# Other numbers for the planner of the heads, four gate blocks early and four held back, and a bank of its own for the last product

## The chip, the cores and the metric

The kernel runs on one core of a Trainium2 chip. The metric is the device time of one execution in microseconds; smaller is better. Before the change the median of three runs is 1488.58 us (1488.05 to 1491.75). One further execution was profiled; every duration below comes from it.

The engines have short names: PE multiplies matrices (PEld is its loading of weights), DVE does vector work, ACT functions and copies, POOL general vector work, and SP issues the DMAs. Each engine takes its instructions in the order in which they were recorded and waits for semaphores in that order.

## The reference

One encoder block for 1024 tokens of width 1024, all in f32:

```
h = rmsnorm(x) * (1 + scale) + shift                # scale, shift, gate from c
bg, cg, ax, az, q, k, v, z, a_raw, b_raw, ga, gb = split(h @ w_in)
ya = (cg * dwconv3(bg * ax) * silu(az)) @ w_pa
q, k, v = silu(dwconv5([q, k, v])); q, k = l2norm(q), l2norm(k)
o = gated_delta(q, k, v, g, beta) forwards + the same backwards     # 8 heads of 128
yb = (rmsnorm(o) * gdn_norm_w * silu(z)) @ w_pb
merged = sigmoid(ga) * ya + sigmoid(gb) * yb
y = rmsnorm(x + gate * (merged @ w_o))
```

`gated_delta` is chunked, and in each chunk it needs the inverse of a unit lower triangular matrix, made from the products of the keys with each other.

## The kernel before

Each f32 product is made of three passes: the weights and the activations are split into a high part (`wh`, `hhi`) and a rest (`wl`, `hlo`), and PE adds hi·hi, lo·hi and hi·lo. A block of 128 columns of `w_in` is thus 48 matmuls of 512 columns, in two halves (`pp_q3_0`, `pp_q3_1` for q of head 3), 24 each. Its weights come by DMA (`wr`), ACT writes `wh`, and POOL subtracts to get `wl` (`load_weights`); an eviction by ACT takes the product from its bank of PSUM (`xpad`).

The program has three parts. First x is normalised and transposed, and the first products are made, to about 102 us of the profile. Then come the eight heads, to about 799 us. The rest is written out by hand: more gate blocks, four groups of Strassen-like pairs of blocks (each pair is seven products, S1 to S4, A11, A12 and A22) with one more pair for the columns of `gb` as the last, and the three products with `w_pa`, `w_pb` and `w_o`.

The heads are recorded by a planner (`Scheduler`). Each head has generators: `prep_k` makes the keys and the matrices N from `gram` (the products of the keys), and issues the inverse; `merge` doubles the inverse's blocks on PE (`psy`, `psu`, `pst`, `psz`, `psv`); `chain` runs the eight steps of the state in both directions (`cb`); `prep_q` and `head_out` do the rest. `chain` and `merge` have the first priority, `prep_k` the second. `fill` is a stream of projections (k, q, v and z of the heads) and eight gate blocks (`ga0` to `ga7`), whose matmuls stand wherever nothing of higher priority is due.

The inverse is the long stretch between gram and psy. DVE makes N and its transposes, DMAs take them through DRAM into a layout for POOL (`s1`, `E`), POOL does 60 small operations that each depend on the one before (`et` and `E`, thirty of each), DMAs bring the result back (`s2`, `N`, `Vb`), DVE and ACT transpose it (`N<-Vb`, `T`, `y`), and `psy` may start.

The planner keeps a time for each engine, estimates each operation's duration (`Engine.cost`), and adds a hop between an operation and one that depends on it: `HOPS['same']` if both are on one engine, other values otherwise. POOL's operations end 0.05 us later for those that depend on them than for the engine itself. It takes what can start first by these numbers; among what is waiting on one engine, priority decides. The numbers set only the order, since the hardware's semaphores hold the real dependences.

`fill` decides by `choose` when a gate block is due: `START` of the eight stand first, and the last blocks, at most `RESERVE`, are kept for places where no projection may go. With the numbers of before, six blocks stand early and two at the end.

In the last pair (`Pair`, `place = "last"`, order S2, S1, S3, A22, A11, A12, S4) each product accumulates in a bank given by its name, `BANK`; S1 and S4 share one of the pool `pc`, and A12 has a bank of `po`, a pool of two.

Of the kernel before, what the change touches and what calls it, by code (L numbers as in the profile page):

```python
# [8 lines left out]
F32 = mybir.dt.float32  # L9
F32R = mybir.dt.float32r  # L10
AF = mybir.ActivationFunctionType
ALU = mybir.AluOpType
# [9 lines left out]
NEG = -1.0e30  # L22

A_BG, A_CG, A_X, A_Z, Q0, K0, V0, Z0, G_A, G_B = (8 * i for i in range(10))
START = 6
RESERVE = 3
PLAIN = (0, 4)
LAST = 6
AHEAD = 5
HOPS = {'same': 0.15, 'other': 0.2, 'from pe': 0.4, 'to pe': 0.35}  # L30
ORDER = "x0 b x1 x2 x3 k0 a0 x4 x5 x6 x7 q0 a1 v0 a2 a3 a4 a5 a6 a7".split()
SPLIT = 2
XS = 'apvapvav'
# [1 line left out]
LW = "gg"  # L35
# [19 lines left out]
class Scheduler:  # L55
# [19 lines left out]
        self.prio = before  # L75

    def hop(self, a, b):
        return HOPS["same" if a == b else "from pe" if a == "pe" else "to pe" if b == "pe" else "other"]

    def after(self, engine, *ends):  # L80
        return max((t + self.hop(e, engine) for d in ends for e, t in d.items()), default=0.0)
# [178 lines left out]
class Engine:  # L260
# [5 lines left out]
    def cost(self, op, outs, ins, kw):  # L266

        n = outs[0].free_size() / 1000.0
        if self._name == "dma":
            size = min(outs[0].nbytes(), ins[0].nbytes())  # L270
            return max(0.4, size / 360e3), 2.4 + size / 500e3
        if self._name == "act":
            pointers = sum(isinstance(kw.get(k), bass.AP) for k in ("bias", "scale"))
            return 0.1 + 0.83 * n + 0.07 * pointers + 0.12 * (len(outs) > 1), 0.08
        if self._name == "pool":
            if ALU.pow in kw.values():
                return 1.7, 0.1
            return (0.31 + 1.95 * n if "tensor" in op else 0.06 + 0.7 * n), 0.05
        if op == "transpose":
            return 0.16 + 1.1 * n, 0.03  # L280
        both = sum(i.space != PSUM and i.free_size() == outs[0].free_size() for i in ins) > 1
        fast = op in ("tensor_copy", "tensor_scalar", "memset") and ins and ins[0].space != PSUM
        return 0.07 + 0.06 * (op == "scalar_tensor_tensor") + (0.66 if fast else 1.2 if both else 1.04) * n, 0.07

    def __getattr__(self, op):
        real = getattr(self._engine, op)
# [14 lines left out]
def block(ctx: ExitStack, tc: tile.TileContext, x, cT, wada, wadag, badaT, nwT, win, wab, cva, cvq,  # L301
# [3 lines left out]
    V, S, G, Q = (Engine(sched, n, e) for n, e in (("dve", nc.vector), ("act", nc.scalar), ("pool", nc.gpsimd),  # L305
                                                   ("dma", nc.sync)))

    def pool(name, bufs, **kw):
        return ctx.enter_context(tc.tile_pool(name=name, bufs=bufs, **kw))
# [5 lines left out]
    pc = pool("pc", 2, space=PSUM)  # L315
    po = pool("po", 2, space=PSUM)
# [24 lines left out]
    def ch(c, w=P):  # L341
        return slice(w * c, w * c + w)
# [13 lines left out]
    def tile_of(pl, shape, tag, name, bufs, dtype=F32):  # L356
        return "tile", pl, shape, tag, name, bufs, dtype

    def urgent():
        return sched.priority(0)  # L360
# [16 lines left out]
    def load_weights(pl, src, name, tag="w", spare=None):  # L377
        hi = yield tile_of(pl, [P, KT * P], f"{tag}hi", f"wh_{name}", 2, F32R)
        lo = yield tile_of(pl, [P, KT * P], f"{tag}lo", f"wl_{name}", 2, F32R)
        for q in range(2):  # L380
            if spare is None:
                raw = yield tile_of(wp, [P, 512], "wraw", f"wr_{name}_{q}", 2)
            else:
                if q == 0:
                    whole = yield staged(spare, f"wr_{name}")
                raw = whole[:, ch(q, 512)]
            with sched.priority(1):
                Q.dma_start(raw, src[:, ch(q, 512)])
                S.activation(hi[:, ch(q, 512)], raw, AF.Copy)
                (G if LW[q] == "g" else V).tensor_tensor(lo[:, ch(q, 512)], raw, hi[:, ch(q, 512)].bitcast(F32), ALU.subtract)  # L390
        weights[name] = hi, lo
        yield "mark", ("w", name)

    def loader(i=0, n=None):
        while n is None or i < n:
            yield "need", ("want", i)
            if wanted[i] is None:
                return
            yield from load_weights(wp, *wanted[i])
            i += 1  # L400
# [12 lines left out]
    def staged(tag, name, dtype=F32):  # L413
        return tile_of(hp, [P, T], tag, name, 1, dtype)
# [26 lines left out]
    with tc.tile_pool(name="st", bufs=1) as st:  # L441
# [172 lines left out]
        def first_weights():  # L614
            for n, name, spare in ((K0, "k0", "hlo5"), (Q0, "q0", "hhi4"), (V0, "v0", "hlo4")):
                yield "need", name
                yield from load_weights(wp if n == V0 else st, win[n], name, "w" if n == V0 else "f", spare)
            yield want(win[K0 + 1], "k1")
# [455 lines left out]
    def fill():  # L1074
# [14 lines left out]
        def choose():  # L1089
            share = (total - START - RESERVE) * (mains - len(jobs)) / mains + START  # L1090
            if gates and jobs and total - len(gates) < int(share):
                return gates.pop(0)
            if jobs and (len(gates) <= RESERVE or all(n in sched.done for n in jobs[0][3])):
                return jobs.pop(0)
            return gates.pop(0) if gates else None
# [18 lines left out]
    V, S, G, Q, PE = nc.vector, nc.scalar, nc.gpsimd, nc.sync, nc.tensor  # L1114

    def bank(pl, name):
        return pl.tile([P, 512], F32, tag="b", name=name)
# [11 lines left out]
    def product(w, mhi, mlo, half, name, order=tuple(range(KT))):  # L1129
        ps = bank((pp, pg)[half], f"pp_{name}_{half}")  # L1130
        for i, k in enumerate(order):
            wh, wl = (t[:, ch(i)] for t in w)
            sl = ch(half, 512)
            PE.matmul(ps, wh, mhi[k][:, sl], start=i == 0, stop=False)  # L1134
            PE.matmul(ps, wh, mlo[k][:, sl], start=False, stop=False)  # L1135
            PE.matmul(ps, wl, mhi[k][:, sl], start=False, stop=i == KT - 1)  # L1136
        return ps
# [31 lines left out]
    BANK = {"S2": pg, "A11": pp, "S1": pc, "S3": pg, "A12": pp, "A22": pg, "S4": pc}  # L1169
# [15 lines left out]
    class Pair:  # L1185
# [31 lines left out]
            self.ops[n] = hi, lo  # L1217

        def product(self, n):
            pl = po if (self.place, n) in (("first", "S4"), ("last", "A12")) else BANK[n]  # L1220
            first = pl not in self.banks
            if first:
                self.banks[pl] = bank(pl, f"ps_{self.name}_{n}")
            ps = self.banks[pl]
            hi, lo = self.ops.pop(n)
            for m in range(4):
                mh, ml = hop[RHS[n]][m]
                for i, (w, r) in enumerate(((hi, mh), (hi, ml), (lo, mh))):
                    PE.matmul(ps, w[:, ch(m)], r, start=first and m == i == 0, stop=m == 3 and i == 2,  # L1229
                              skip_group_check=True)  # L1230
            self.after(n, ps)
# [8 lines left out]
        def after(self, n, ps):  # L1240
            u = self.u
            if self.place == "last":
                if n in ("S2", "S3"):
                    self.temp({"S2": "u2", "S3": "u3"}[n], ps, None)
                elif n == "A11":
                    self.temp("e1", ps, None)
                    V.tensor_tensor(u["u3"], u["u3"], u["e1"], ALU.add)
                    self.consume(1, 1, self.banks[pc], u["u3"])
                    self.consume(1, 0, self.banks[pg], u["e1"])
                    V.tensor_tensor(u["u2"], u["u2"], u["e1"], ALU.add)  # L1250
                elif n == "A12":
                    self.consume(0, 0, ps, u["e1"])
                elif n == "S4":
                    self.consume(0, 1, ps, u["u2"])
                return
            first = self.place == "first"
            if n == "A11":
                self.temp("e1", ps, None)
            if n == ("S2" if first else "A11"):
                self.temp("u2", self.banks[pg], u["e1"])  # L1260
                if first:
                    V.tensor_tensor(u["u2"], self.banks[po], u["u2"], ALU.add)
            if n == "S3":
                self.temp("u3", ps, u["e1"])
                self.consume(1, 1, self.banks[pc], u["u3"])
            elif n == "A12":
                self.consume(0, 0, ps, None)
            elif n == "A22":
                self.consume(1, 0, ps, u["e1"])
            elif n == ("S1" if first else "S4"):  # L1270
                self.consume(0, 1, ps, u["u2"])
# [95 lines left out]
    for i, (p, n) in enumerate(steps):  # L1367
        if i + AHEAD < len(steps):
            q, k = steps[i + AHEAD]
# [139 lines left out]
    for n in range(2):  # L1509
        for t in range(8):  # L1510
            if n == 0:
                load_wo(1, t)
            pl = (pp, pg)[t % 2]
# [81 lines left out]
```

## Time and profile before

| | |
|---|---|
| median of three runs | 1488.58 us |
| profiled execution | 1486.97 us |
| its span on the core | 1485.2 us |
| mean granted clock of PE | 0.981 |
| first part ends, heads end | about 102 and 799 us |
| POOL, the 240 `E` and 240 `et` | 120.0 and 114.3 us |

The span is what the profile shows from the first instruction to the last. A row of a view names the line, the engine, the operation, and out<-in by the program's names without buffer numbers. An idle time is put down to the event that ended it. `engine, number` with an `x` behind it is busy time and the count of instructions; the granted clock is 1.00 at full speed.

### The profile page before, as it was taken

What the parts mean: (1) busy time and instruction counts of PE and PEld (TensorE: products, weight loads), DVE (VectorE), ACT (ScalarE), POOL (GpSimd) and SP (SyncE); (2) the same over time, 40 slices, a digit from 0 to 9 for tenths busy, and PEclk for the clock granted to TensorE, in tenths of its full rate; (3) what the DMA queues carried; (4) which work ended last, traced back from release to release, by engine and by line L of the source; (5) the groups of instructions that cost most, each with busy time, mean ns of one, the idle gap of its engine ahead of it and who ended that gap; (6) DMA issues with size and microseconds to landing.
All of it is one profiled execution on the core that took longest, in us unless ns stands there. A gap on an engine that the chain in (4) does not pass through costs nothing.

```text
span 1485.2 us, 22649 instructions
## 1 busy us (share of the span) xinstructions
PE 1402.8 (94%) x8526; PEld 1161.1 (78%) x8526; DVE 858.9 (58%) x1466; ACT 614.0 (41%) x1495; POOL 691.8 (47%) x864
## 2 busy tenths in 40 slices
PE   5799999899999999996899999999999899999998
PEld 4687878787878787875788877787878677788886
DVE  7959327467767657476525566565756446623335
ACT  5227728546565647464434323232222431222211
POOL 6103748462768473575404745454454312255301
PEclk9899999999999999997999999999999999999999
DMA  8204351312342412323112320303030557565502
GB/s 322 94 29 138 105 134 56 86 39 84 114 97 82 115 44 50 105 71 89 29 44 86 113 79 22 114 15 128 15 113 30 190 188 239 197 199 169 193 15 100
DMA packets 123582, 153.37 MB, mean 103 GB/s; under 512 B 74705, under 2 KB 75089, under 8 KB 123473
## 3 DMA queue, kind: packets, MB, share of 16 engines
q1 hardware_dynamic: 123184, 151.14, 32.0%
q8 instruction: 67, 1.10, 0.3%
q10 hardware_dynamic: 288, 0.79, 0.1%
q14 instruction: 43, 0.34, 0.1%
HBM read 122.40 MB, written 29.49 MB: 102 GB/s over the span
## 4 chain that ended last, share of the span: by engine, by line
PE 67%; DVE 12%; POOL 8%; ACT 5%; DMA 4%; issue 2%; SPq 1%; POOLq 0%; ACTq 0%; DVEq 0%
PE pp_ga L204 6%; PE cb L204 4%; PE pp_q L204 4%; PE pp_k L204 4%; PE ps_ax_S L1229 4%; PE ps_cg_S L1229 3%; POOL E L295 3%; POOL et L295 3%; PE o L204 3%; PE ps_bg_S L1229 3%; PE ps_az_S L1229 2%; PE pp_pb L1134 2%; PE pp_pb L1135 2%; PE pp_pb L1136 2%; PE fo L1501 2%
## 5 line engine op out<-in xcount | busy, mean ns | idle before, releaser
L295 POOL TENSOR_TENSOR E<-E,et 128x30 f32<-128x30 f32 (+7 forms) x240 | 120.0, 500 | 16.6
L295 POOL TENSOR_TENSOR et<-E 128x30 f32<-128x30 f32 (+7 forms) x240 | 114.3, 476 | 27.5 <-DMA E<-s 10.8
L295 ACT ACTIVATE vw<-cb,cols 128x128 f32<-128x128 f32 x112 | 34.9, 363 | 92.0 <-PE cb L204 91.8
L295 DVE SCALAR_TENSOR_TENSOR S<-S,exps,cb 128x128 f32<-128x128 f32 x96 | 29.2, 343 | 69.8 <-PE cb L204 69.5
L1126 POOL TENSOR_TENSOR wl_pa<-wr_pa,wh_pa 128x512 fp32r<-128x512 f32 x16 | 20.4, 1295 | 86.6 <-ACT wh_pa L1125 86.6
L295 ACT ACT_TABLE_LOAD x42 | 53.9, 1283 | 1.4 <-PEq L1590 0.8
L295 POOL TENSOR_TENSOR wl_ga<-wr_ga,wh_ga 128x512 fp32r<-128x512 f32 x16 | 23.2, 1455 | 65.9 <-ACT wh_ga L295 65.8
L204 PE MATMUL pp_z<-hlo,wh_z 128*128 128x512 f32 x128 | 53.1, 415 | 0.0
L204 PE MATMUL pp_z<-hhi,wh_z 128*128 128x512 f32 x128 | 52.9, 413 | 0.0
L204 PE MATMUL pp_z<-hhi,wl_z 128*128 128x512 f32 x128 | 52.6, 411 | 0.0
L204 PE MATMUL pp_ga<-hhi,wh_ga 128*128 128x512 f32 x128 | 51.2, 400 | 1.5 <-ACT xpad L295 1.5
L204 PE MATMUL pp_ga<-hhi,wl_ga 128*128 128x512 f32 x128 | 51.5, 402 | 0.0
L204 PE MATMUL pp_ga<-hlo,wh_ga 128*128 128x512 f32 x128 | 51.1, 399 | 0.0
L1134 PE MATMUL pp_pb<-bhi,wh_pb 128*128 128x512 f32 x128 | 50.6, 396 | 0.0
L1136 PE MATMUL pp_pb<-bhi,wl_pb 128*128 128x512 f32 x128 | 50.6, 395 | 0.0
L1135 PE MATMUL pp_pb<-blo,wh_pb 128*128 128x512 f32 x128 | 50.6, 395 | 0.0
L1134 PE MATMUL pp_pa<-yhi,wh_pa 128*128 128x512 f32 x128 | 50.5, 395 | 0.0
L1136 PE MATMUL pp_pa<-yhi,wl_pa 128*128 128x512 f32 x128 | 49.9, 390 | 0.0
L1135 PE MATMUL pp_pa<-ylo,wh_pa 128*128 128x512 f32 x128 | 49.9, 389 | 0.0
L204 PE MATMUL pp_q<-hhi,wl_q 128*128 128x512 f32 x112 | 46.7, 417 | 2.1 <-POOL wl_q L295 2.1
L295 DVE SCALAR_TENSOR_TENSOR r<-cb,negeg,vp 128x128 f32<-128x128 f32 x112 | 34.0, 344 | 23.7 <-PE cb L204 23.4
L295 DVE SCALAR_TENSOR_TENSOR qT<-xpad,cvq_t,qT 128x1024 f32<-128x1024 f32 x32 | 47.2, 1474 | 0.5
(806 smaller groups left out, 4660.7 us busy)
## 6 DMA issues: line engine op xcount, KB each, us to landing
wada<-in_wada SPq DMA_DIRECT2D x16, 512.0 KB, 7.1
D<-gr_d SPq DMA_DIRECT2D x16, 512.0 KB, 7.7
xt<-in_x SPq DMA_DIRECT2D x8, 512.0 KB, 7.6
wr_k<-in_win SPq DMA_DIRECT2D x16, 256.0 KB, 3.1
wr_q<-in_win SPq DMA_DIRECT2D x16, 256.0 KB, 3.8
wr_v<-in_win SPq DMA_DIRECT2D x16, 256.0 KB, 4.7
wr_ga<-in_win SPq DMA_DIRECT2D x16, 256.0 KB, 3.2
qg<-er_d SPq DMA_DIRECT2D x8, 512.0 KB, 5.3
```

The source lines that it names most:

```text
L204: getattr(self.pe, what)(out, *ins, **kw)
L295: self._sched.record(self._name, lambda: real(*args, **kw), outs, ins, cost, extra, table, op == "memset")
L1126: G.tensor_tensor(lo[:, ch(q, 512)], raw, hi[:, ch(q, 512)].bitcast(F32), ALU.subtract)
L1134: PE.matmul(ps, wh, mhi[k][:, sl], start=i == 0, stop=False)
L1135: PE.matmul(ps, wh, mlo[k][:, sl], start=False, stop=False)
L1136: PE.matmul(ps, wl, mhi[k][:, sl], start=False, stop=i == KT - 1)
L1229: PE.matmul(ps, w[:, ch(m)], r, start=first and m == i == 0, stop=m == 3 and i == 2, skip_group_check=True)
L1501: PE.matmul(ps, mhi[k][:, ch(t)], wl, start=False, stop=k == KT - 1)
```

## The change

The planner's numbers and two spots of code change; the arithmetic stays, apart from the order of one sum.

```
-START = 6
-RESERVE = 3
+START = 4
+RESERVE = 4
...
-HOPS = {'same': 0.15, 'other': 0.2, 'from pe': 0.4, 'to pe': 0.35}
+HOPS = {'same': -0.05, 'other': 0.2, 'from pe': 0.4, 'to pe': 0.35}
...
     def hop(self, a, b):
-        return HOPS["same" if a == b else "from pe" if a == "pe" else "to pe" if b == "pe" else "other"]
+        if a == b and a != "dma":
+            return HOPS["same"]
+        return HOPS["from pe" if a == "pe" else "to pe" if b == "pe" else "other"]
...
-        return 0.07 + 0.06 * (op == "scalar_tensor_tensor") + (0.66 if fast else 1.2 if both else 1.04) * n, 0.07
+        return 0.07 + 0.06 * (op == "scalar_tensor_tensor") + (0.66 if fast else 1.16 if both else 1.04) * n, 0.07
...
-                (G if LW[q] == "g" else V).tensor_tensor(lo[:, ch(q, 512)], raw, hi[:, ch(q, 512)].bitcast(F32), ALU.subtract)
+                with urgent():
+                    (G if LW[q] == "g" else V).tensor_tensor(lo[:, ch(q, 512)], raw, hi[:, ch(q, 512)].bitcast(F32), ALU.subtract)
...
-            pl = po if (self.place, n) in (("first", "S4"), ("last", "A12")) else BANK[n]
-            first = pl not in self.banks
+            own = (self.place, n) in (("first", "S4"), ("last", "A12"), ("last", "S4"))
+            pl = po if own else BANK[n]
+            first = own or pl not in self.banks
...
                     V.tensor_tensor(u["u2"], u["u2"], u["e1"], ALU.add)
+                    V.tensor_tensor(u["u2"], self.banks[pc], u["u2"], ALU.add)
```

Two dependent operations of one engine now have no gap in the plan (two DMAs count as different engines); a DVE operation on two SBUF tensors counts a little less; the `wl` subtraction has the first priority; and four gate blocks stand early, four are held back. In the last pair S4 no longer accumulates upon S1's bank but starts its own, and a DVE addition brings S1's sum into `u2`, which is later added to S4.

The planner moves much of the heads' order. Three places of it follow. The first is PE at the merge of head 7, where psy7 begins and psu7 follows it. Before, psy7 stood behind the last matmuls of z6, and up to psu7 there were only transposes of head 6's output (`otp6`):

```order
L204 MATMUL pp_z6_1_7412<-hhi7_621,wh_z6_6934 128x512
L204 MATMUL pp_z6_1_7412<-hlo7_622,wh_z6_6934 128x512
L204 MATMUL pp_z6_1_7412<-hhi7_621,wl_z6_6935 128x512
L204 MATMUL psy7_7550<-T64_7_7082,N0_7_6479 32x32
...
L204 MATMUL psy7_7550<-y64_7_7083,N1_7_6480 32x32
L204 MATMUL otp6_0_7589<-ident_72,vp6_6506 128x128 x4
L204 MATMUL otp6_1_7595<-ident_72,vp6_6506 128x128 x2
L204 MATMUL psu7_7599<-N0_7_6479,Vb7_7008 32x32 x2
```

Now the gate block `ga4` stands around it:

```order
L206 MATMUL pp_ga4_0_7498<-hlo1_106,wh_ga4_7396 128x512
L206 MATMUL pp_ga4_0_7498<-hhi1_102,wl_ga4_7397 128x512
L206 MATMUL pp_ga4_0_7498<-hhi2_103,wh_ga4_7396 128x512
L206 MATMUL psy7_7511<-T64_7_6877,N0_7_6367 32x32
...
L206 MATMUL psy7_7511<-y64_7_6878,N1_7_6368 32x32
L206 MATMUL pp_ga4_0_7498<-hlo2_107,wh_ga4_7396 128x512
L206 MATMUL pp_ga4_0_7498<-hhi2_103,wl_ga4_7397 128x512
L206 MATMUL pp_ga4_0_7498<-hhi3_104,wh_ga4_7396 128x512
L206 MATMUL pp_ga4_0_7498<-hlo3_108,wh_ga4_7396 128x512
L206 MATMUL pp_ga4_0_7498<-hhi3_104,wl_ga4_7397 128x512
L206 MATMUL pp_ga4_0_7498<-hhi4_509,wh_ga4_7396 128x512
L206 MATMUL psu7_7554<-N0_7_6367,Vb7_6876 32x32 x2
```

Six wide matmuls now stand between psy7 and psu7, and `ga4` to `ga7` go on beside the rest of merge 7 and chain 7.

The second place is ACT at the third and fourth gate block, early in the heads. `wh_ga3` is the high part of the weights of block 3, `xpad<-pp_ga2_1` the eviction of the second half of block 2, D the decay matrices of head 1. Before:

```order
L295 ACTIVATE xpad0_116<-pp_ga1_1_1228 128x512
L295 ACTIVATE sqj_884,kss1_902<-ktp1_0_1284 128x128 x4
L295 ACTIVATE wh_ga3_1294<-wr_ga3_0_1296 128x512
L295 ACTIVATE ktok1_901<-ktp1_1_1305 128x512
L295 ACTIVATE sqj_884,kss1_902<-ktp1_1_1305 128x128 x4
```

and now:

```order
L297 ACT_TABLE_LOAD
L297 ACTIVATE xpad1_117<-pp_ga2_1_1368 128x512
L297 ACT_TABLE_LOAD
L297 ACTIVATE D1_1_905<-D1_1_905,neggc_122 128x128
L297 ACTIVATE wh_ga3_1309<-wr_ga3_0_1311 128x512
L297 ACTIVATE wh_ga3_1309<-wr_ga3_1_1312 128x512
```

`wh_ga3` stood behind the eviction of block 1; it now stands behind that of block 2. On PE the matmuls of block 3 directly follow block 2's.

The third place is POOL in the inverse of head 3. Leaving out `E` and `et`, before there stood among its sixty operations:

```order
L295 MEMSET E3_3519 64x16
...
L295 TENSOR_TENSOR wl_v3_3645<-wr_v3_0_3646,wh_v3_3644 128x512
...
L295 TENSOR_TENSOR wl_z2_3902<-wr_z2_0_3903,wh_z2_3901 128x512
...
L295 TENSOR_TENSOR oss2_3922<-oss2_3922,pos_half_78 128x8
...
L295 TENSOR_TENSOR kss4_3906<-kss4_3906,pos_half_78 128x8
...
L295 TENSOR_TENSOR wl_q4_4026<-wr_q4_0_4027,wh_q4_4025 128x512
...
L295 MEMSET E3_3519 64x16 x2
```

and now:

```order
L297 MEMSET E3_3301 64x16
...
L297 TENSOR_TENSOR wl_v3_3555<-wr_v3_0_3556,wh_v3_3554 128x512
...
L297 MEMSET E3_3301 64x16 x2
L297 TENSOR_TENSOR wl_z2_3814<-wr_z2_0_3815,wh_z2_3813 128x512
L297 TENSOR_TENSOR wl_z2_3814<-wr_z2_1_3816,wh_z2_3813 128x512
L297 TENSOR_TENSOR oss2_3806<-oss2_3806,pos_half_78 128x8
L297 TENSOR_TENSOR kss4_3818<-kss4_3818,pos_half_78 128x8
L297 TENSOR_TENSOR wl_q4_3937<-wr_q4_0_3938,wh_q4_3936 128x512
```

Each `wl` comes in two halves, of which the second isn't shown where "..." stands. Before, six of these subtractions and two powers stood inside the inverse; now two subtractions do, and the others follow it. Between the last gram of head 3 and psy3 PE had 228 matmuls of 512 columns and 120 of 128; now it has 156 and 114. For heads 4 to 7 the new counts are 166 to 175 and 106, where they were 179, 197, 241 and 144 of the wide ones and 106 to 122 of the narrow.

## The prediction

> **What bounds the kernel now.** I read the page's first two parts, then the waits of PE, then windows cut where those waits lie, then the timeline at one wait and the chain of one head.
>
> ```profile
> span 1485.2 us, 22649 instructions
> PE 1402.8 (94%) x8526; PEld 1161.1 (78%) x8526; DVE 858.9 (58%) x1466; ACT 614.0 (41%) x1495; POOL 691.8 (47%) x864
> PEclk9899999999999999997999999999999999999999
> ```
>
> PE is busy for 1402.8 of 1485.2 us, no other engine for more than 58%. So time can only be won or lost in PE's idle 82.4 us and where its clock is down, above all near the 19th digit of the clock. The waits of PE say what it stood for:
>
> ```profile
> PE psz L204 <- ACT T L295: 7.3, 3, 5.6
> PE psy L204 <- DVE N L295: 5.2, 1, 5.2
> PE cb L204 <- ACT vn L295: 3.9, 3, 1.7
> PE psy L204 <- DVE T L295: 3.5, 1, 3.5
> PE ps_gb_S L1229 <- DVE gb L1332: 2.8, 1, 2.8
> PE pp_q L204 <- POOL wl_q L295: 2.1, 2, 1.1
> ```
>
> The columns are the total, how often, and the longest. psy, psu, psz and psv are the steps by which a head's inverse is merged, cb the state chain of a head, ps_gb_S a product of the last Strassen pair. In the next view each row is a stretch of time: its length, then the busy time of PE, PEld, DVE, ACT and POOL, the granted clock, and DMA.
>
> ```profile
> 255.00:272.00 17.00, 11.61 (x73) 10.17 (x72) 9.67 (x30) 12.94 (x33) 7.99 (x22) 0.90 0.29 47
> 272.00:667.00 395.00, 380.57 (x3189) 324.42 (x3190) 258.28 (x527) 227.11 (x683) 235.80 (x375) 0.99 0.29 80
> 667.00:740.00 73.00, 54.02 (x577) 46.49 (x575) 43.31 (x90) 36.39 (x109) 38.03 (x73) 0.86 0.28 67
> 740.00:799.00 59.00, 58.74 (x469) 50.21 (x470) 19.19 (x57) 21.42 (x63) 9.04 (x6) 0.94 0.14 46
> 671.60:688.60 17.00, 7.75 (x204) 6.45 (x205) 13.63 (x23) 7.16 (x15) 5.76 (x11) 0.50 0.74 180
> 736.40:746.60 10.20, 8.02 (x182) 6.05 (x184) 7.31 (x19) 2.36 (x6) 3.53 (x3) 0.50 0.08 29
> 1180.20:1183.60 3.40, 3.40 (x10) 2.66 (x9) 0.87 (x2) 0.97 (x2) 0.00 (x0) 0.50 1.03 416
> ```
>
> The heads' tail, 667 to 740, holds 73.00 − 54.02 = 19.0 us of idle time, where the 395 us ahead of it hold 14.4. There the merges of heads 6 and 7 have little projection work beside them. Clock 0.50 marks three stretches in which PE's work takes twice as long. A pause costs twice: the wait, then half of the busy time behind it.
>
> **The change, part by part.**
>
> **1. Four gate blocks held back instead of two.** Blocks 4 and 5 (96 matmuls each) leave the early stage; four now stand around merge 7 and chain 7, as the order shows, and head 6's merge gets the projections that stood there. At most this wins the tail's 19.0 us and half of the busy time at half clock, (7.75 + 8.02)/2 = 7.9: **26.9 us**. What the merges there still wait for is charged in parts 4 and 5.
>
> **2. End of chain 0.** From 255 to 272 PE is idle for 17.00 − 11.61 = 5.4 us: the last steps of chain 0 have no fill between them, and vn comes late. In the new order z0's matmuls stand between these steps. I take all: **5.4**, at least 0.
>
> **3. The last pair.** The timeline there (start, duration, engine, tiles; the bracket is idle time and releaser):
>
> ```profile
> 1176.49 0.58 ACT L1236 ACTIVATE e_gb<-ps_gb_A 128x512 f32<-128x512 f32 x1
> 1177.11 1.37 DVE L1247 TENSOR_TENSOR u_gb<-u_gb,e_gb 128x512 f32<-128x512 f32 x1 [10.90 <-ACT e_gb L1236]
> 1178.58 0.69 DVE L1332 TENSOR_TENSOR gb<-ps_gb_S,u_gb 128x512 f32<-128x512 f32 x1
> 1179.33 0.50 PE L1229 MATMUL ps_gb_S<-hhi,whS_gb 128*128 128x512 f32 x1 [2.81 <-DVE gb L1332]
> ```
>
> S4 accumulates in a bank that the 1178.58 row still reads. With its own bank (the pool has two, and A12 takes the other) the 2.81 us go, and with them half of the 3.40 us at clock 0.50: 1.7. Together **4.5**; nothing is late next, since the weights and hi/lo operands of S4 stood ready. The added addition is one DVE row of 0.69 us; DVE had idled 10.90 us, and if that cover were gone it would cost those 0.69.
> The 2.81-us wait is shorter than the idle window of about 3.4 us which the Trainium skill, TensorE: Matmul & The Clock Gate, What's actually happening, names as what throttles the array. By that page 2.8 us would be won here; the row at clock 0.50 right behind the wait differs, and the sum goes by the row.
>
> **4. No gap on one engine, and the urgent lo parts.** The planner used to reckon 0.20 us between two dependent operations of one engine (its hop of 0.15 and 0.05 behind POOL's end); now 0. Sixty such POOL operations (E and et) make a head's inverse, so psy is planned some 12 us earlier against them. By the order, PE's work from the last gram of a head to its psy was 228 wide (512 columns) and 120 narrow matmuls in head 3, and is now 156 and 114; in heads 4 to 7 it is 166 to 175 and 106. How long these last, and what the inverse needs, head 3 shows:
>
> ```profile
> L204 PE MATMUL gram<-kT x16: 271/275/275, 359.9 to 362.2; 128*128 128x128 f32 x16
> 377.71 0.88 POOL L295 TENSOR_TENSOR et<-E 128x30 f32<-128x30 f32 x1 [1.18 <-DMA E<-s]
> 430.11 0.23 POOL L295 TENSOR_TENSOR E<-E,et 128x15 f32<-128x15 f32 x1
> 440.06 1.78 DVE L295 STREAM_TRANSPOSE N<-Vb 32x256 f32<-32x256 f32 x4 [0.90 <-DMA Vb<-s]
> 443.71 0.21 PE L204 MATMUL psy<-T,N 32*32 32x32 f32 x1
> 439.67 0.39 PE L204 MATMUL pp_q<-hlo,wh_q 128*128 128x512 f32 x1
> 439.90 0.39 PE L204 MATMUL pp_q<-hhi,wl_q 128*128 128x512 f32 x1
> ```
>
> Wide matmuls start 0.23 us apart. gram ends at 362.2 + 0.275 = 362.5 and psy starts at 443.7: 81.2 us for 228 × 0.23 = 52.4 and 120 narrow ones, so 0.24 each. The new distance of head 3 is then 156 × 0.23 + 114 × 0.24 = **63.2 us**; it is 56 to 66 in the others, by their counts.
> The need: from gram's end to the first et 377.7 − 362.5 = 15.2; from the last E (430.3) to the last transpose (441.8) 11.5; between them the sixty operations, their gaps and the lo parts (wl) placed among them. The windows of the inverses of heads 0, 3 and 4 and the sum over all eight, all engines (columns as above):
>
> ```profile
> 150.20:204.50 54.30, 54.30 (x249) 44.40 (x249) 11.06 (x31) 30.95 (x76) 37.09 (x74) 1.00 0.26 89
> 376.30:430.50 54.20, 51.13 (x292) 43.63 (x291) 41.55 (x81) 36.13 (x108) 46.87 (x71) 0.99 0.21 71
> 443.20:487.70 44.50, 43.71 (x472) 37.75 (x471) 33.28 (x58) 25.33 (x83) 38.30 (x69) 1.00 0.25 86
> sum 388.90, PE 376.95 PEld 324.15 DVE 232.02 ACT 219.95 POOL 305.88; mean PE 47.12 PEld 40.52 DVE 29.00 ACT 27.49 POOL 38.23
> ```
>
> The same with the E and et operations alone:
>
> ```profile
> 150.20:204.50 54.30, 23.10 (x63) 1.00 0.26 89
> 376.30:430.50 54.20, 35.44 (x63) 0.99 0.21 71
> 443.20:487.70 44.50, 31.40 (x62) 1.00 0.25 86
> sum 388.90, POOL 235.74; mean POOL 29.47
> ```
>
> E takes 29.5 us on average, 23.1 to 35.4; other POOL work among it (305.88 − 235.74)/8 = 8.8 us. In the new order heads 2 to 5 have two lo parts there, about 2.5 us. Gaps are some 4 us (head 4: 44.50 − 38.30 = 6.2, with its first wait for E). The need is 15.2 + 29.5 + 4 + 2.5 + 11.5 = **62.7 us against 63.2**: hardly any slack on average, where the order of before left 70 to 98 in all heads but the last. With E between its two ends PE would wait 0 to 5.4 us at psy (15.2 + 35.4 + 18.0 − 63.2); I take 1.5 a head, **12 us**, as an estimate between the two rows, and **4** more because heads 0, 6 and 7 keep four or five lo parts in the chain. Half clock behind two or three of these waits: **4**. The ends are 0 (E as in head 0) and 8 × 5.4 + 4 = 47 with 8 × 1.7 = 14 for the clock.
> GPSIMD Engine Reference, Key points, of the Trainium skill says that GpSimd shares its SBUF interfaces with VectorE and suffers from DVE instructions with two SBUF inputs, which speaks against packing a head tighter. The two rows agree: E took 23.1 us beside 11.06 us of DVE work and 35.4 beside 41.55. By it, E would go to the upper end, and the sum to the third rival below.
> The urgent lo parts of q now precede the chains; the 2.1 us of pp_q <- wl_q go: **2.1**.
>
> **5. What the new order loses.** Gate block 3 follows block 2 on PE directly, but on ACT its wh stands behind the eviction of block 2 and two table loads.
>
> ```profile
> L295 ACT ACT_TABLE_LOAD x42 | 53.9, 1283 | 1.4 <-PEq L1590 0.8
> L295 ACT ACTIVATE xpad<-pp_ga x12: 580/598/602, 136.9 to 202.7; 128x512 f32<-128x512 f32 x12
> L295 ACT ACTIVATE wh_ga<-wr_ga x10: 614/620/632, 129.9 to 180.9; 128x512 fp32r<-128x512 f32 x10
> L295 POOL TENSOR_TENSOR wl_ga<-wr_ga,wh_ga x11: 1284/1296/2329, 119.1 to 182.7; 128x512 fp32r<-128x512 f32 x11
> 272.50:284.40 11.90, 9.43 (x247) 7.15 (x246) 5.00 (x18) 5.30 (x21) 5.58 (x16) 1.00 0.71 197
> ```
>
> Eviction 0.60, table 1.28, one D operation of about 0.4 and wh 0.62 make 2.9; the third matmul needs wl 1.30 later, with two matmuls between: 3.9 us, and 1.7 for half clock behind it: **5.6** (lower end 0, if block 2's eviction could run early, which its place behind PE excludes). Merges 0 and 7 have as little work between their steps as merge 1 had, whose window lost 11.90 − 9.43 = 2.5: **5.0** for two. Order in stage 1 hardly moves; I cost it at 0, ±2.
>
> **The sum.** Won 26.9 + 5.4 + 4.5 + 2.1 = 38.9; lost 12 + 4 + 4 + 5.6 + 5.0 = 30.6. Net **−8.3 us**. The profiled execution took 1486.97, its span and 1.8 us around it, and lies 1.6 below the median of 1488.58; the median goes to **1480**.
>
> **The rivals.**
> - *All is kept.* E runs at 26 us, as a quiet DVE allows; only parts 5 and 4's four us stay: 38.9 − 14.6 = 24 won, **1464**. For it: head 0's 23.1. Against: the mean.
> - *Given back.* Psy waits of 2.3 us a head (18 us, 6 for the clock) and the rest as above: 38.6 lost, net 0, **1488**.
> - *The inverse is late in every head.* E at 33.4 makes the need 66.6, a wait of 3.4 in each of eight heads, 27 us, with 4 for the lo parts, 14 for the clock and 10.6 of part 5: 56 lost, 17 more than won, **1506**. It decides from about 2.3 us a head (E above 32.3): then it is slower than before. For it: head 3's 35.4; against: a PE that waits leaves DVE idle too, and E quicker.
> - *The bank does not help:* if S4 still waited, 4.5 us less would be won; the order shows S4 directly behind A12 with nothing of DVE to read its bank.
>
> **How the numbers follow.** Forecast 1480 (own range 1472 to 1488) 0.40; all kept 0.22; given back 0.14; late inverse 0.24. 0.3%, 4.5 us, is what a measurement tells from no change. Faster: 0.22 and 0.31 of the forecast, **0.53**; same: 0.09 of the forecast, 0.10 and 0.02 of the others, **0.21**; slower **0.26**. The range runs from just below the first rival to just above the third: **1462 to 1508**.
>
> **What would show it.** Right: no PE wait above 3 us from 667 to 740, none at the last product, PE waits "psy <- DVE N" or "T" in several heads of 1 to 3 us, one of about 4 us at pp_ga <- ACT wh_ga early. Wrong: psy waits above 3 us in most heads with E above 32.3 us (slower), or none at all (1464); a gate block that leaves the tail uncovered would bring back part 1's idle time.

## The result, and the profile after

The changed kernel takes **1506.9 us** (median of four runs, 1503.9 to 1508.0) against 1488.3 for the kernel before beside it: a ratio of 1.0117, 95% interval [1.0096, 1.0139]. It is 1.2% slower. The forecast of 1480 us was wrong; the time is that of the third rival, "the inverse is late in every head" (1506 us, chance 0.24), and lies just inside the range.

The page of the changed kernel, its first two parts:

```profile
span 1502.1 us, 22636 instructions
PE 1409.6 (94%) x8526; PEld 1164.2 (78%) x8526; DVE 856.0 (57%) x1467; ACT 612.3 (41%) x1493; POOL 678.8 (45%) x864
PEclk9999899999999999999999999999999999999999
```

The span is 16.9 us longer: PE idles 92.5 us where it idled 82.4, and is busy for 6.8 us more with the same matmuls, which is work at half clock. The weak spot has moved from the 19th digit of the clock to the fifth, that is from the tail to the stretch before merge 0. The five largest waits of PE among the heads of the changed kernel:

```profile
PE ktp L206 <- ACT kT L297: 8.3, 2, 5.1
PE cb L206 <- DVE S L297: 7.5, 3, 6.6
PE psy L206 <- ACT sqj L297: 7.3, 1, 7.3
PE otp L206 <- DVE vp L297: 5.6, 3, 2.7
PE pp_ga L206 <- ACT wh_ga L297: 5.0, 1, 5.0
```

The wait of the last product (ps_gb_S <- DVE gb, 2.8 us) and those of pp_q for wl_q are gone, as forecast, and the wait at gate block 3 (pp_ga <- ACT wh_ga) has come. But only one of the new waits is at psy. The others are at ktp (transposed keys of a later head), cb and otp: operations of quite other work. Stretch by stretch, cut where the merges of heads 0, 1, 5 and 7 end, before and then after:

```profile
102.00:229.00 127.00, 125.16 (x792) 102.12 (x792) 70.18 (x114) 70.64 (x160) 60.48 (x102) 1.00 0.44 130
229.00:284.00 55.00, 47.06 (x487) 40.61 (x487) 37.24 (x93) 42.91 (x128) 37.15 (x70) 0.97 0.27 68
284.00:583.00 299.00, 287.07 (x2473) 245.28 (x2470) 205.16 (x416) 175.01 (x528) 178.62 (x285) 0.99 0.27 76
583.00:750.00 167.00, 147.73 (x1239) 125.85 (x1237) 96.02 (x194) 84.13 (x244) 89.96 (x150) 0.92 0.28 75
```

```profile
99.00:203.00 104.00, 96.08 (x642) 76.78 (x642) 62.54 (x103) 66.79 (x149) 49.04 (x81) 0.95 0.39 112
203.00:273.00 70.00, 59.12 (x556) 51.02 (x552) 44.42 (x100) 40.23 (x129) 44.29 (x73) 0.93 0.30 79
273.00:592.00 319.00, 295.05 (x2469) 250.15 (x2464) 202.89 (x416) 173.93 (x527) 173.73 (x300) 0.96 0.28 76
592.00:762.00 170.00, 161.16 (x1296) 136.23 (x1296) 93.61 (x195) 89.39 (x250) 87.72 (x149) 0.97 0.28 77
762.00:821.00 59.00, 56.13 (x322) 48.44 (x322) 21.31 (x49) 20.66 (x62) 11.51 (x8) 1.00 0.19 63
```

Length minus PE's busy time is idle time: before 1.8, 7.9, 11.9, 19.3 us, after 7.9, 10.9, 24.0, 8.8 and, in the gate blocks at the end, 2.9. The clock falls with it (0.99 to 0.96 in the third stretch). So the tail did win, and the early and middle heads lost more.

What it costs can be counted by adding to the idle time half of PE's busy time at clock 0.50. Here are the sums by stretch, for the profiled execution of each kernel that follows (the experiments are told below; the last column is from merge 7 to the end of the heads and gate blocks):

| kernel | to merge 0 | merge 1 | merges 2 to 5 | merges 6, 7 | rest | sum |
|---|---|---|---|---|---|---|
| before | 1.8 | 9.5 | 15.0 | 27.2 | 0.0 | 53.5 |
| changed | 11.8 | 14.1 | 34.3 | 13.9 | 2.9 | 77.0 |
| gate blocks 4/4 alone (e3) | 16.4 | 8.0 | 15.3 | 24.1 | 0.0 | 63.8 |
| changed, old hops (e1) | 16.1 | 4.2 | 25.3 | 19.7 | 0.0 | 65.3 |
| changed, POOL's gap kept (e2) | 11.4 | 4.6 | 18.6 | 8.5 | 4.3 | 47.4 |
| changed, narrow inverse (e5) | 11.0 | 8.1 | 21.7 | 6.5 | 4.4 | 51.7 |
| POOL's gap kept, gate blocks 6/2 (e6) | 8.9 | 4.7 | 20.5 | 6.2 | 1.3 | 41.6 |

The sums of the first two rows differ by 23.5 us. Less the 4.5 us that the bank of the last product wins behind the heads, that is 19.0, where the spans differ by 16.9.

**How a late inverse stops work that does not need it.** Head 3 is the plain case. The first row is the list of gram's instructions, the others are from the timeline. On POOL the last E ends at 399.8, and PE stands at psy:

```profile
L206 PE MATMUL gram<-kT x16: 272/275/275, 343.3 to 345.0; 128*128 128x128 f32 x16
361.79 0.24 POOL L297 TENSOR_TENSOR et<-E 128x30 f32<-128x30 f32 x1 [1.04 <-DMA E<-s]
399.54 0.23 POOL L297 TENSOR_TENSOR E<-E,et 128x15 f32<-128x15 f32 x1
404.97 0.43 DVE L297 STREAM_TRANSPOSE T<-N 32x256 f32<-32x256 f32 x1 [6.59 <-DMA N<-s]
407.99 1.79 DVE L297 STREAM_TRANSPOSE N<-Vb 32x256 f32<-32x256 f32 x4 [1.41 <-DMA Vb<-s]
407.99 0.84 ACT L297 ACTIVATE T<-Vb 32x256 f32<-32x256 f32 x2 [8.51 <-DMA Vb<-s]
411.27 0.19 ACT L297 ACTIVATION_READ_ACCUMULATOR sqj<-ktp 128x1 f32 x1
411.51 0.25 PE L206 MATMUL psy<-T,N 32*32 32x32 f32 x1 [7.31 <-ACT sqj L297]
```

PE had come to psy at 404.2, and the last transpose ended at 409.8. The releaser is given as sqj, the squares of a later head's keys, which ACT makes from ktp. That fits the program: psy and ktp take their banks from one pool of two, and on ACT the reading of ktp stood behind the transposes T, for which ACT had waited 8.51 us. So the last 1.7 us before psy went to the bank, which was late for the same reason. In head 1 the same lateness is put down to something else, in the timeline of DVE and PE:

```profile
252.11 0.88 DVE L297 STREAM_TRANSPOSE T<-N 32x256 f32<-32x256 f32 x2 [7.26 <-DMA N<-s]
254.94 1.78 DVE L297 STREAM_TRANSPOSE N<-Vb 32x256 f32<-32x256 f32 x4 [0.55 <-DMA Vb<-s]
256.76 0.60 DVE L297 SCALAR_TENSOR_TENSOR S<-S,exps,cb 128x128 f32<-128x128 f32 x2
257.16 1.22 PE L206 MATMUL cb<-S,kT 128*128 128x128 f32 x4 [6.60 <-DVE S L297]
```

S, a step of chain 0, needs nothing of the inverse. But DVE takes its instructions in order, the plan had put the transposes T ahead of S, and while DVE waited 7.26 us for the inverse's DMA, S and with it PE waited too. The next way leads over POOL's own queue:

```profile
563.48 1.65 POOL L297 TENSOR_TENSOR oss<-oss,pos_half 128x8 f32<-128x8 f32 x1
565.16 0.31 DVE L297 TENSOR_SCALAR vp<-vp,oss 128x128 f32<-128x128 f32 x1 [4.51 <-POOL oss L297]
572.62 1.97 PE L206 MATMUL ktp<-ident,kT 128*128 128x128 f32 x8 [5.07 <-ACT kT L297]
```

oss, a power for the output of head 4, stands on POOL behind the last E of head 5, which ended at 563.5. DVE waits for it at vp, the convolutions of kT stand behind vp, and PE at last waits 5.07 us for kT. Over the whole program the changed kernel's view of DVE's waits has

```profile
DVE vp L297 <- POOL oss L297: 19.1, 7, 6.8
```

where before it had

```profile
DVE vp L295 <- POOL oss L295: 8.1, 4, 2.9
```

### The profile page after: what moved, and what is told of

Same layout as the page of the kernel before. It is cut to its first block, busy times and chain, and to the rows that moved or that the text cites. A ratio compares the mean times of both kernels' runs of the same rounds, so it can differ in the third digit from the quotient of the medians.

```text
span 1502.1 us, 22636 instructions
## 1 busy us (share of the span) xinstructions
PE 1409.6 (94%) x8526; PEld 1164.2 (78%) x8526; DVE 856.0 (57%) x1467; ACT 612.3 (41%) x1493; POOL 678.8 (45%) x864
## 4 chain that ended last, share of the span: by engine, by line
PE 44%; DVE 7%; POOL 2%; ACT 2%; issue 1%; POOLq 0%; ACTq 0%
PE ps_ax_S L1233 3%; PE ps_cg_S L1233 3%; PE pp_ga L206 3%; PE ps_bg_S L1233 3%; PE ps_az_S L1233 2%; PE pp_pb L1137 2%; PE pp_pb L1138 2%; PE pp_pb L1139 2%; PE fo L1506 2%; PE fo L1504 2%; PE fo L1505 2%; DVE ga L1438 2%; PE pp_gb L1137 1%; PE pp_gb L1138 1%; PE pp_gb L1139 1%; PE ps_ax_A L1233 1%
## 5 line engine op out<-in xcount | busy, mean ns | idle before, releaser
L297 POOL TENSOR_TENSOR E<-E,et 128x30 f32<-128x30 f32 (+7 forms) x240 | 109.6, 457 | 17.8
L297 DVE SCALAR_TENSOR_TENSOR N<-gram,cols,D 128x128 f32<-128x128 f32 x128 | 34.6, 342 | 48.1 <-PE gram L206 48.1
L297 POOL TENSOR_TENSOR wl_q<-wr_q,wh_q 128x512 fp32r<-128x512 f32 x16 | 24.0, 1504 | 77.9 <-ACT wh_q L297 71.6
```

The costliest lines, as they stand in the source:

```text
L297: self._sched.record(self._name, lambda: real(*args, **kw), outs, ins, cost, extra, table, op == "memset")
```

## The experiments

All twelve kernels ran beside the kernel before; its median was 1487.5 to 1488.6 us in the three groups. Theory L is the third rival: the plan counts no gap between POOL's sixty operations, so the inverse comes late. The rivals are G, that the places of the gate blocks cost the time, and U, the urgent lo parts.

**e1, all hops of before** in the changed kernel:

```
-HOPS = {'same': -0.05, 'other': 0.2, 'from pe': 0.4, 'to pe': 0.35}
+HOPS = {'same': 0.15, 'other': 0.2, 'from pe': 0.4, 'to pe': 0.35}
...
+        return HOPS["same" if a == b else "from pe" if a == "pe" else "to pe" if b == "pe" else "other"]
```

> The changed kernel with the hops of before (same engine 0.15) and all else of the change. Theory L (the inverse comes late because the plan counts no gap between POOL's sixty operations): the blocked waits of the heads go, and the gates and the bank win in the tail, so faster than before: 1465 to 1480 us. Rival G (the gate blocks' places cost the time): still 1500 us or more. Rival U (the urgent lo parts): still above 1495 us.

1493.0 us, ratio to before 1.0030 [1.0016, 1.0044]. 14 us better than the change and still not better than before: none of the three gets its number. The hops do cost, but something else of the change does too.

**e2, the gap on POOL alone** in the changed kernel:

```
-            return (0.31 + 1.95 * n if "tensor" in op else 0.06 + 0.7 * n), 0.05
+            return (0.31 + 1.95 * n if "tensor" in op else 0.06 + 0.7 * n), 0.25
```

> The changed kernel, in which only POOL's operations end 0.25 us later for what depends on them (0.05 before), so that two of POOL stand 0.20 apart in the plan as before the change, while DVE and ACT keep no gap. Theory L: as good as with all old hops, within 6 us of it, 1468 to 1483 us. If the missing gaps of DVE and ACT cost the time instead: above 1495 us.

1476.8 us, 0.9925 [0.9899, 0.9951]: 30 us less than the change, by one number on POOL. The time is in the range that theory L gave, though not because it equals e1: it is 16 us better. So the missing gap splits in two. On POOL it costs 30 us; on DVE and ACT it wins. (The 16 us are not quite theirs alone. The later end counts for every engine that waits for POOL, so e2 also plans what other engines do behind POOL 0.20 us later than e1, and two dependent DMAs 0.05 us later.)

**e3, the gate blocks alone**, in the kernel before:

```
-START = 6
-RESERVE = 3
+START = 4
+RESERVE = 4
```

> The kernel before with START 4 and RESERVE 4 alone. Theory L and the prediction's parts 1 and 2: the tail's idle 19 us and its half clock go, some 5 to 10 us are lost at gate block 3 and elsewhere: 1462 to 1480 us. Rival G: slower than before, 1495 us or more.

1499.9 us, 1.0081 [1.0058, 1.0103]. That is rival G's number, and it speaks against part 1 of the prediction. In the table, merges 6 and 7 lose 24.1 instead of 27.2, and the stretch to merge 0 16.4 instead of 1.8. What PE waited for most in this kernel's heads:

```profile
PE psz L204 <- ACT T L295: 7.7, 2, 4.2
PE psy L204 <- DVE T L295: 5.8, 2, 4.0
```

One of these two psz waits (3.6 us at 226.6) and one psy wait (1.8 at 215.3) are in merge 0, where before PE waited for 0.3 us.

**e4, the own bank alone**, in the kernel before (the diff's last two pieces):

> The kernel before with the own bank of the last product alone. The prediction's part 3: 4.5 us less, 1484 us, and no wait of PE at the last product. By the page of the notes 2.8 us less. If the bank does not help: 1488.5 us and the 2.81-us wait is still there.

1482.7 us, 0.9962 [0.9951, 0.9974], that is 3.9 to 7.3 us won. No wait of PE is left from 1170 to 1184. Part 3's 4.5 us holds; the 2.8 us of the bare wait lie below the interval, so the half clock behind it was part of the price.

**e5, the same order with a shorter inverse.** Every instruction stands where it stood in the changed kernel. POOL's sixty operations work on a quarter of their columns while the plan still counts them all, and N is scaled by 0.001; most of the inverse is left out:

```
+            w = (n + 3) // 4
+            G._n = m * n / 1000.0
...
+            G.tensor_tensor(E[:, 0:m, p + 1 : p + 1 + w], E[:, 0:m, p + 1 : p + 1 + w], tt, ALU.add)
...
-        V.tensor_scalar(nbk, bk, -1.0, None, ALU.mult)
+        V.tensor_scalar(nbk, bk, -1.0e-3, None, ALU.mult)
```

> The changed kernel with its order kept instruction by instruction, in which POOL's sixty operations of each inverse work on a quarter of their columns (the plan still counts them at full width) and the keys' matrix N is scaled by 0.001; so the inverse is left out for the most part. Theory L: the inverse ends some 8 to 10 us sooner in each head, the waits of 3 to 7 us from head 1 to head 6 go, and the heads' loss (idle and half clock) falls from 77 to about 50 us: 1475 to 1485 us. Rival G (places of the gate blocks and the order as such): above 1497 us.

1475.9 us, 0.9913 [0.9887, 0.9939]: 31 us less in the same order (24.9 between the two profiled executions, which the table follows). The sum over the eight windows of the inverse, E alone, in the changed kernel and then in this one:

```profile
sum 309.50, POOL 222.29; mean POOL 27.79
```

```profile
sum 270.90, POOL 165.36; mean POOL 20.67
```

E is 7.1 us shorter a head, but the way from the first et to the last E only 4.8 (309.50 and 270.90 over eight), not the 8 to 10 expected. The waits shrink to these, where the changed kernel had 7.5 at cb, 7.3 at psy and 8.3 at ktp; the wait at gate block 3, which has nothing to do with the inverse, stays at 5.0, and only those of psz for T grow, from 4.5:

```profile
PE cb L206 <- DVE S L297: 4.3, 5, 3.2
PE psy L206 <- ACT sqj L297: 1.3, 1, 1.3
PE ktp L206 <- ACT kT L297: 1.1, 2, 0.8
PE pp_ga L206 <- ACT wh_ga L297: 5.0, 1, 5.0
PE psz L206 <- DVE T L297: 8.2, 4, 2.4
```

This decides for theory L: with the order fixed, a shorter inverse alone moves the time by 31 us. How much the same shortening would win in the order of before, no run shows.

**e6, POOL's gap kept and the gate blocks as before** (e2 with START 6, RESERVE 3):

> POOL's gap of 0.20 as in the faster version (1476.8 us), but START 6 and RESERVE 3 as before the change. If the two held-back blocks help beside that plan: slower than it, 1482 to 1490 us, with idle time back in the merges of heads 6 and 7. If they only move the loss to merge 0: within 5 us of it, 1472 to 1481 us, with under 5 us lost up to merge 0 and 25 us from merge 6 on.

**1466.7 us**, 0.9850 [0.9823, 0.9878]: better than both kernels, and 10 us better than e2. No expectation had this. Merges 6 and 7 lose 6.2 us with only two blocks held back, so the four held back were not what covered the tail.

**e7, five early, three late** (e2 with START 5, RESERVE 3):

> POOL's gap of 0.20, five gate blocks early and three held back. If the loss at merge 0 (11 us) goes with one more early block and the tail stays covered by three: 1466 to 1473 us. If the places only trade: 1474 to 1480 us.

1484.4 us, 0.9972 [0.9959, 0.9986]: above both ranges, and 8 and 18 us worse than its neighbours e2 and e6. Merge 1 alone loses 15.1 us in its profile. A small change of the plan's numbers reshuffles the whole list, so a difference of this size between two orders can be chance of the order.

**e8, lo parts not urgent** (e2 without `with urgent()`):

> POOL's gap of 0.20 as in the faster version, with the lo parts at their old priority. If the urgent lo parts matter: 1485 us or more, with waits of PE for wl. If not: within 5 us of 1476.8 us.

1477.2 us, 0.9913 [0.9883, 0.9943], 0.3 us from e2: the urgent lo parts matter neither way where POOL's gap is kept, and rival U is out.

**e9, old hops with the gate blocks as before** (e1 with START 6, RESERVE 3):

> Six gate blocks early as before, all hops of before, and the rest of the change (own bank, urgent lo parts, the DVE cost). If the gain of the 1466.7 us version comes from counting no gap on DVE and ACT: 1480 to 1486 us, the own bank's share alone, with the tail's idle time back (over 12 us from merge 5 to merge 7). If it comes from the urgent lo parts or the DVE cost: 1465 to 1475 us.

1479.6 us, 0.9942 [0.9923, 0.9961], just below the first range and above the second. Against e6 it differs only in the hops: no gap on DVE and ACT is worth 13 us there, with the reservation made at e2. Against e4 it differs in the urgent lo parts and the DVE cost. It is 3 us faster (1479.6 and 1482.7), so together these two do not make the kernel slower there.

**e10, the change with START 6 and RESERVE 3**:

> The change as it is, with no gap on any engine, but START 6 and RESERVE 3. If the two losses add (late inverse 30 us, gate blocks 10 us): 1494 to 1500 us. If the late inverse costs only beside four early blocks: below 1485 us.

1511.1 us, 1.0150 [1.0131, 1.0169]. Neither: the losses do not add. With a late inverse the early blocks win nothing back. The way over POOL's queue is still there in DVE's waits, and at the end of the heads PE has run out of fill and waits 9.4 us for the last chain's output:

```profile
DVE vp L297 <- POOL oss L297: 24.4, 6, 7.1
```

**e11 and e12, other gaps on POOL** (e6 with 0.15 and 0.35 in place of 0.25, that is gaps of 0.10 and 0.30):

> As the 1466.7 us version, with 0.10 us between two dependent POOL operations in the plan. That is near to what they take on the chip (0.08 us beside the plan's 0.48). Theory L with scatter from head to head (a late inverse stops PE, an early one costs nothing): slower than with 0.20, 1470 to 1480 us. If only the mean counts: 1462 to 1468 us.

> As the 1466.7 us version, with 0.30 us between two dependent POOL operations in the plan. Theory L: the inverse waits nowhere, but psy is planned later than it need be and the tail grows: 1466 to 1476 us. If the inverse is still late with 0.20: below 1463 us.

1474.5 us, 0.9911 [0.9891, 0.9931], and 1468.5 us, 0.9867 [0.9851, 0.9882]. With six early blocks the times by gap are 1511.1 (none), 1474.5 (0.10), 1466.7 (0.20) and 1468.5 us (0.30). A step of 0.10 is 6 us in the planned length of each inverse. None at all is 37 to 44 us worse than the other three. The gap nearest to what the chip shows, 0.10, is 8 us worse than 0.20, and another 6 us too many cost 2. Both times lie in theory L's ranges, but e7 moved by as much through the order alone, so the 8 us do not show that more than the mean counts.

In one table, medians in us:

| gap between dependent operations | 4 early, 4 late | 6 early, 2 late |
|---|---|---|
| all hops of before | 1493.0 (e1) | 1479.6 (e9) |
| none on DVE and ACT, 0.20 on POOL | 1476.8 (e2) | 1466.7 (e6) |
| none on any engine | 1506.9 (the change) | 1511.1 (e10) |

## Why the prediction was wrong, point by point

**Two terms of the sum were mis-sized.** The time came out 27 us above the forecast. About 10 of them are part 4: it charged the inverse 12 + 4 + 4 = 20 us, and e2, which differs from the change by POOL's gap alone, shows 30. The other 17 are the gains: without part 4 the sum had 38.9 − 10.6 = 28.3 us to win, and e2, where the inverse is no longer late, won 10.7 (1487.5 − 1476.8). Most of that is part 1: it gave itself 26.9 us of the tail, and e2's tail lost 8.5 + 4.3 instead of 27.2, that is 14.4 less. Either miss alone would have taken the forecast gain away.

**Part 4, the inverse, failed by its size.** Its mechanism, an inverse that comes late, was right, but not all the places where that stops PE. It said that the need (62.7 us) and PE's distance (63.2) were about equal, and took 12 + 4 us of waits and 4 of clock. e2 and e5 show 30 and 31 us. Head 3, of which the estimate was made, shows where the rest was. These rows are its way from gram to where PE comes to psy, before and after, and its E alone:

```profile
362.50:443.70 81.20, 78.13 (x436) 66.49 (x435) 55.19 (x118) 44.85 (x131) 49.63 (x74) 0.98 0.36 92
345.30:404.20 58.90, 58.31 (x352) 50.57 (x350) 32.93 (x68) 29.94 (x92) 41.49 (x71) 1.00 0.33 95
360.50:399.90 39.40, 30.31 (x63) 1.00 0.23 80
```

*The distance:* PE came to psy 404.2 − 345.3 = 58.9 us after gram, not 63.2. The 0.24 us for a narrow matmul were got by dividing all of head 3's 81.2 us before by its matmuls; but in that stretch PE had idled 81.20 − 78.13 = 3.1 us and lost 0.02 × 81.2 = 1.6 to the clock. A distance taken over waits hides the waits. (The rows count 436 and 352 matmuls, so the narrow ones are 208 and 196, not the 120 and 114 counted ahead of the prediction; that hurts little, since both counts are short by the same share. Without the 4.7 us a narrow one takes (76.5 − 52.4) / 208 = 0.116 us, and the new distance comes to 156 × 0.23 + 196 × 0.116 = 58.6.) *The need:* from gram's end to the first et it took 361.8 − 345.3 = 16.5 us, and from the last transpose's end another 1.7 to psy, which the prediction had left out. It was 411.5 − 345.3 = 66.2 in all, with E at 30.3, so 7.3 us late. *The places:* the prediction let the inverse stop PE only at psy. DVE's in-order queue (S behind T) and POOL's (oss behind E) stopped PE at cb, ktp and otp as well; waits that it could have found by asking what is queued behind each of the inverse's instructions. So its own signs of a late inverse, psy waits above 3 us in most heads and E above 32.3, did not come either. How much each way costs was not separated by a run.

The price of E was not the error. Over the eight windows the changed kernel has, for all engines,

```profile
sum 309.50, PE 295.54 PEld 256.12 DVE 164.79 ACT 166.74 POOL 261.78; mean PE 36.94 PEld 32.02 DVE 20.60 ACT 20.84 POOL 32.72
```

E took 27.8 us on average where 29.5 was reckoned, beside DVE work of 164.79 in 309.5 us (53%) where before it was 60%. Within the changed kernel it took 22.3 us in head 0, beside 3.74 us of DVE work in 35.70, and 32.9 in head 1, beside 27.94 in 42.70. That goes with what GPSIMD Engine Reference, Key points, of the Trainium skill says of the shared SBUF interface, and against its use in the prediction: the tighter plan did not put more DVE work beside E.

**Part 1, the held-back blocks: wrong, and the larger miss.** It gave them all of the tail's 26.9 us. In the changed kernel the tail lost 13.9 + 2.9 instead of 27.2, so 10.4 were won. Alone the blocks won 3.1 of it (e3, 24.1 against 27.2) and lost 14.6 before merge 0. The tail was covered by the order that counts no gap on DVE and ACT: with two blocks held back it loses 6.2 us (e6), with the old hops and the same places 17.3 (e9, by the same count as the table: 5.9 in the stretch of merge 6 and 11.4 in that of merge 7). The prediction saw waits go with blocks in the order's rows and did not ask whether the blocks or the order did it.

**Part 2, chain 0's end:** 5.4 us were to go. In the changed kernel merge 1's stretch lost 14.1 instead of 9.5, since the late inverse of head 1 stops S there; with POOL's gap it is 4.6 and 4.7 (e2, e6). So that stretch gains 4.8 to 4.9 once the inverse is not late.

**Part 3, the bank:** right; 4.5 forecast, 3.9 to 7.3 measured alone, and the wait gone. A wait of 2.81 us, shorter than the idle window of about 3.4 us that the Trainium skill gives (TensorE: Matmul & The Clock Gate, What's actually happening), was thus followed by half clock, and both went together.

**Part 4's lo parts:** the waits of pp_q went, but e8 shows that the priority did not matter to the time.

**Part 5:** the wait at gate block 3 came where it was worked out, 5.0 us and 0.85 for wl where 3.9 was reckoned. The timeline of the changed kernel has the chain that the order showed. The prediction names two table loads but its sum has one; the other stands ahead of the eviction, behind D operations that kept ACT 0.8 us beyond block 2's last matmul (164.4 to 165.2):

```profile
165.22 1.28 ACT L297 ACT_TABLE_LOAD   x1
166.51 0.60 ACT L297 ACTIVATE xpad<-pp_ga 128x512 f32<-128x512 f32 x1
167.13 1.28 ACT L297 ACT_TABLE_LOAD   x1
168.42 0.40 ACT L297 ACTIVATE D<-D,neggc 128x128 f32<-128x128 f32 x1
169.39 0.79 PE L206 MATMUL pp_ga<-hhi,wh_ga 128*128 128x512 f32 x1 [5.01 <-ACT wh_ga L297]
```

With its half clock the stretch to merge 0 lost 11.8 us, 10.0 more than before; 5.6 + 2.5 had been charged. Merge 7 had been charged another 2.5, which the tail's figures above include.

**The sum and the chances.** The third rival had the mechanism and the time, the latter partly by chance: E was not at its 33.4 us, and part 1 won less than it reckoned. Its threshold of 2.3 us a head was passed by the waits of heads 1, 3, 4, 5 and 7 (6.6, 7.3, 3.2, 5.1 and 2.7 us; 24.9 together, 3.1 a head over eight, where it had 27). The forecast rested on a balance of 62.7 against 63.2, each known to some 5 us, and on waits that can only lose; the chance of 0.24 was too small for that.

## What to carry to other kernels

A planner should count a long dependent chain on the long side: of four planned lengths 6 us apart the third and fourth, which count it longer than the chip takes, gave 1467 and 1468 us, the first 1511, because a late result at the head of an in-order queue stops all that is planned behind it. Correct one engine's numbers at a time, since the same number was right for DVE and ACT (13 to 16 us won) and wrong for POOL (30 to 44 lost). Ask of a wait that goes in a new order which of the changes took it away. When a wait moves, list what stands behind each instruction of the late chain on its engine, and take the pace of an engine from stretches without waits.

## What the runs showed of the hardware that was not expected

A 2.81-us wait of PE was enough for 3.4 us at clock 0.50 (kernel before), and removing it won 5.7 us [3.9, 7.3] where the wait alone is 2.8. Shorter pauses had the same behind them: in the kernel before, PE stood from 575.9 to 577.8, and the clock fell 1.6 us later.

```profile
577.80 0.39 PE L204 MATMUL psz<-T,N 64*64 64x64 f32 x6 [1.90 <-DVE T L295]
579.41:582.82 3.41, 3.41 (x29) 2.66 (x29) 3.34 (x14) 2.30 (x4) 1.30 (x2) 0.50 0.27 84
```

POOL's small operations follow each other at 0.07 to 0.08 us beyond their own duration even when each needs the one before (361.79 + 0.24 to 362.11 in the changed kernel), which over sixty operations is 4 to 5 us.
